# Encoder trunk on one core: gate-table eviction as a pipeline of half blocks, v's first slab ahead of the table, two half slabs of values prepared ahead

## The chip, the core and the metric

The kernel runs on one core of one Trainium2 chip. The metric is device time in microseconds for one execution, the median of three runs. TensorE (PE) multiplies, ScalarE (ACT) and VectorE (DVE) split operands and evict results, SyncE (SP) issues the loads, and ScalarE issues the stores of the gate table. In the profile's rows PEld is TensorE's weight load.

## What is computed

Two layers on a sequence of 256 tokens of width 1024 (`x` is 256 x 1024, float32): a mixer (an HGRN2 recurrence in layer 0, an RG-LRU block in layer 1), each followed by a PEER feed-forward part, which is what the change concerns:

```python
def peer_ffn(h, w_q, sub_keys, u_tab, v_tab):
    q = (h @ w_q).reshape(B, S, 8, 2, 128)
    scores = einsum('bshpd,hpkd->bshpk', q, sub_keys)
    s1, i1 = top_k(scores[..., 0, :], 16);  s2, i2 = top_k(scores[..., 1, :], 16)
    cand_s = s1[..., :, None] + s2[..., None, :]        # 256 candidates
    cand_id = i1[..., :, None] * 128 + i2[..., None, :]
    top_s, top_pos = top_k(cand_s, 16)
    ids, gate = take(cand_id, top_pos), softmax(top_s)
    # per token, 8 heads x 16 experts out of 16384
    act = gelu(einsum('thkd,td->thk', u_tab[ids], h))
    return einsum('thk,thkd->td', gate * act, v_tab[ids])
```

Every sub-layer has an RMSNorm with shift, scale and gate from a conditioning vector (adaLN).

## The kernel before, in words

The kernel gathers no rows. It computes `gelu(u h)` for all 16384 experts (the u stage), multiplies it by a dense table of gates that is zero outside the chosen experts, and multiplies the result by all of `v_tab` (the v stage). Each of `peer_u` and `peer_v` comes in 64 slabs of 1 MB (128 x 2048 float32). Float32 values are split into a high and a low part, ScalarE writing the high one (line 300) and VectorE the low one (line 301), and each product is three matmuls: 24 matmuls for half a slab in the u stage (lines 308, 309, 311), 12 in the v stage (line 1305).

*Slabs.* An arena of 19 slabs holds the u stage's activations (128 groups of 256 columns, eight groups to a slab, 16 slabs) and the incoming slabs. `order` lists all loads in the order in which they are taken; `pump()` issues the next load on SP's queue as soon as a slab is in `allowed`, and `free(n)` gives a slab back. From u slab 44 on only three slabs are left for loads, until `release` gives back slabs whose activations have been used: three at v slab 18, and in layer 0 five more at v slab 34. SP's queue is in order: a load that waits holds up those behind it.

*Products and side work.* `push(prep, mm, post, cost)` emits the preparation of a half (its split) at once and puts its matmuls into a queue that holds `depth` halves (one) back. When a half's matmuls are emitted, `side(cost)` adds `cost` to a credit and runs steps of the side generators while the credit is positive; each `yield` gives the cost of the step just emitted. In the u stage the side generators are `routing()` (scores, top-16, softmax; VectorE) and then `gmats()`, the gate table; their credit per half is C_ROUTE, then C_G0. What is left when u ends is emitted by `drain_sides()`.

*The gate table.* `gmats` works on 32 blocks of eight tokens. `build(n)` makes one-hot matrices on VectorE (lines 1204 and 1206), `mult(m)` multiplies for half a block (four matmuls, line 1215) into one of three pairs of PSUM banks, and `evict(m)` adds the two halves of the result into a staging tile STG (the tile xT, two buffers): ScalarE copies (line 1222), VectorE adds (line 1223). After a block's second half ScalarE issues the store of 512 KB to `gates` in DRAM (line 1225).

*The v stage.* Before eight v slabs, two slabs `gd` are read back from `gates` (`GLEAD` v slabs ahead; the first two at the start, which wait for the whole table, `tabled`), and `gates()` multiplies them into the activations on VectorE (line 1252). `s2` splits the v slab and one group of 256 activations for each half (lines 1296 and 1297) and multiplies. In layer 0 adaLN slabs are woven in (`ada_slab`, line 394); `load_cond` and `pre_final` broadcast columns through `row_bcast` (lines 374, 375), and `pre_final` transposes (line 1381).

Of the kernel before, what the change touches and what calls it, by code (L numbers as in the profile page):

```python
# [17 lines left out]
OP = mybir.AluOpType  # L18
# [27 lines left out]
C_ROUTE = 1.65  # L46
C_G0 = 2.05
# [25 lines left out]
def body(ctx, tc, A, out):  # L73
# [222 lines left out]

    def split(raw):
        n = wsn[0] % NWS
        wsn[0] += 1
        ACT.activation(WS[:, n, 0], raw, AF.Copy)  # L300
        V.tensor_tensor(WS[:, n, 1], raw, WS[:, n, 0], op=OP.subtract)  # L301
        return WS[:, n, 0], WS[:, n, 1]
# [85 lines left out]
    def ada_slab():  # L388
        n, raw = take("ada")
        i, s = order[n][1:]  # L390
        for m in range(2):
            col = 2 * s + m
            r_ = raw[:, m * 1024:(m + 1) * 1024]
            V.scalar_tensor_tensor(r_, r_, 1.0, cb, op0=OP.mult, op1=OP.mult, accum_out=mod[:, i, col:col + 1])  # L394
        free(n)
        if s % 4 == 3:
            c0 = 2 * (s - 3)
            V.tensor_tensor(mod[:, i, c0:c0 + 8], mod[:, i, c0:c0 + 8],
                            sv("b_ada")[:, i * 48 + c0:i * 48 + c0 + 8], op=OP.add)
            if c0 == 40:  # L400

                V.tensor_scalar(mod[:, i, c0:c0 + 8], mod[:, i, c0:c0 + 8], 1.0 / GS16, None, op0=OP.mult)

    def weaved():
        while st["taken"] < len(order) and order[st["taken"]][0] == "ada":
            ada_slab()
# [607 lines left out]
    def peer(i):  # L1014
# [179 lines left out]
        def gmats():  # L1194

            P2 = pool.tile([P, 2, NTB, 2, P], F16, name="gsplit", tag="gsplit")

            def build(n):
# [4 lines left out]
                for dst, t_ in ((EQ, T2), (P1[:, bf], T1)):  # L1203
                    V.tensor_tensor(pairs(dst), pairs(io1[:, None, :].to_broadcast([P, NTB, P])), spread(t_),  # L1204
                                    op=OP.is_equal)
# [12 lines left out]
            def evict(m):  # L1218
                b = 2 + 2 * (m % 3)
                pv = PS[:, b:b + 2].rearrange("p a (t g j) -> p g j (a t)", t=2, g=2)  # L1220
                st_ = STG[:, m // 2 % 2, :, m % 2 * 4:m % 2 * 4 + 4]
                ACT.activation(st_, pv[:, 0], AF.Copy)  # L1222
                V.tensor_tensor(st_, pv[:, 1], st_, op=OP.add)  # L1223
                if m % 2:
                    nc.scalar.dma_start(Gd[i][:, :, m // 2],
                                        STG[:, m // 2 % 2].rearrange("p (q j) t -> p q (j t)", q=8))

            for n in range(S // NTB):
                build(n)
                yield 2.7  # L1230
                if n:
                    evict(2 * n - 2)
                    yield 0.7
                mult(2 * n)
                if n:
                    evict(2 * n - 1)
                    yield 0.7
                mult(2 * n + 1)
            yield 1.0
            for m in (S // 4 - 2, S // 4 - 1):  # L1240
                evict(m)
                yield 0.7
            tabled.add(i)
            pump()

        def gates():

            n, raw = take("gd")
            q, th = order[n][2] // 2, order[n][2] % 2
            av = slabs(aslab(16 * q), 2).rearrange("p a (j t) -> p (a j) t", t=S)[:, :, th * P:(th + 1) * P].rearrange(  # L1250
                "p j (g t) -> p j g t", t=8)
            V.tensor_tensor(av, av, raw.rearrange("p (g j t) -> p j g t", g=16, t=8), op=OP.mult)  # L1252
            free(n)
# [4 lines left out]
        def s2(cost):  # L1258
            n, raw = take("v")
            g = order[n][2]  # L1260
            if g == 63 and i == 1:
# [22 lines left out]
            for half in range(2):  # L1284
# [41 lines left out]
        if i == 0:  # L1326
            sides.append(cond)
            sides.append(softplus())
        for it in vs[i]:
            if it[0] == "ada":  # L1330
                settle(cond)
                weaved()
                continue
            if it[0] == "gd":
                gates()
# [4 lines left out]
            elif g == 18:  # L1340
                release(0, 1, 2)
            elif g == 34 and i == 0:
                release(3, 4, 5, 6, 7)
            elif g == 52 and i == 0:
                reserve(0, 1, 2, 3, 4, 5, 6)
            elif g == 58 and i == 0:
                release(13)
            s2(C_G1)
            if g == 63 and i == 1:
                flush()  # L1350
            if i == 1 and g == 44:
                sides.append(pre_final())
        if i == 0:
# [156 lines left out]
```

## Time and profile before

| | |
|---|---|
| median of 3 runs | 2033.39 us (2030.5 to 2035.17) |
| profiled execution | 2030.43 us, of which its span is 2028.6 |
| granted TensorE clock, mean | 0.986 |
| busy: TensorE, VectorE, ScalarE | 1943.8, 1571.2, 1004.0 us |
| moved by DMA | 456.87 MB, 225 GB/s |
| u stages (layer 0, layer 1) | about 250 to 692, 1205 to 1647 us |
| v stages | about 692 to 1070, 1647 to 2016 us |

The span is from the first to the last instruction in the trace. An engine's busy time counts its instructions alone; TensorE's ends are modelled, so holes are read from its waits and from the starts of its matmuls.

### The profile page before, as it was taken

What the parts mean: (1) busy time and instruction counts of PE and PEld (TensorE: products, weight loads), DVE (VectorE), ACT (ScalarE), POOL (GpSimd) and SP (SyncE); (2) the same over time, 40 slices, a digit from 0 to 9 for tenths busy, and PEclk for the clock granted to TensorE, in tenths of its full rate; (3) what the DMA queues carried; (4) which work ended last, traced back from release to release, by engine and by line L of the source; (5) the groups of instructions that cost most, each with busy time, mean ns of one, the idle gap of its engine ahead of it and who ended that gap; (6) DMA issues with size and microseconds to landing.
All of it is one profiled execution on the core that took longest, in us unless ns stands there. A gap on an engine that the chain in (4) does not pass through costs nothing.

```text
span 2028.6 us, 32101 instructions
## 1 busy us (share of the span) xinstructions
PE 1943.8 (96%) x12862; PEld 1781.8 (88%) x12862; DVE 1571.2 (77%) x2797; ACT 1004.0 (49%) x1419; POOL 0.2 (0%) x4
## 2 busy tenths in 40 slices
PE   6999999999999799999999989999999979999998
PEld 6898899999999777888888889999999978888786
DVE  6798659887888677888877776988788866676575
ACT  3544544445555354444445744445455544454454
POOL 0000000000000000000000000000000000000000
PEclk9999999999999899999999999999999989999999
DMA  8654714455767667989753482545676766766561
GB/s 347 271 200 163 285 69 158 175 187 198 238 193 244 210 247 269 394 347 399 290 208 154 158 306 90 185 167 192 208 244 195 235 225 261 290 252 260 203 234 57
DMA packets 125765, 456.87 MB, mean 225 GB/s; under 512 B 7720, under 2 KB 73512, under 8 KB 74672
## 3 DMA queue, kind: packets, MB, share of 16 engines
q1 hardware_dynamic: 59056, 421.28, 55.4%
q10 hardware_dynamic: 66560, 33.56, 5.5%
q8 instruction: 100, 1.64, 0.3%
q14 instruction: 49, 0.40, 0.1%
HBM read 418.10 MB, written 36.70 MB: 224 GB/s over the span
## 4 chain that ended last, share of the span: by engine, by line
PE 88%; DVE 6%; ACT 3%; DMA 2%; issue 1%; SPq 0%; DVEq 0%; ACTq 0%
PE psum L1305 33%; PE psum L311 14%; PE psum L308 14%; PE psum L309 14%; PE psum L1215 3%; PE psum L478 2%; DVE wsplit L301 1%; PE psum L358 1%; DMA arena<-peer_v_dram 1%; PE psum L688 1%; PE psum L318 1%; PE psum L595 1%; ACT wsplit L300 1%; PE psum L1088 1%; PE psum L915 1%
## 5 line engine op out<-in xcount | busy, mean ns | idle before, releaser
L301 DVE TENSOR_TENSOR wsplit<-arena,wsplit 128x1024 fp32r<-128x1024 f32 x600 | 729.7, 1219 | 300.8 <-ACT wsplit L300 298.4
L300 ACT ACTIVATE wsplit<-arena 128x1024 fp32r<-128x1024 f32 x600 | 632.4, 1056 | 492.1 <-PE psum L1305 311.4
L1305 PE MATMUL psum<-wsplit,gsplit 128*128 128x512 f32 x3048 | 703.3, 392 | 19.4 <-ACT gsplit L1296 14.3
L1305 PEld LDWEIGHTS psum<-wsplit,gsplit 128*128 128x128 f32 x3048 | 574.8, 189 | 145.3 <-ACT gsplit L1296 15.4
L308 PE MATMUL psum<-hsplit,wsplit 128*128 128x256 f32 x2448 | 607.7, 286 | 2.1 <-ACT wsplit L300 2.1
L309 PE MATMUL psum<-hsplit,wsplit 128*128 128x256 f32 x2448 | 600.5, 283 | 0.0
L308 PEld LDWEIGHTS psum<-hsplit,wsplit 128*128 128x128 f32 x2448 | 469.1, 192 | 4.3 <-ACT wsplit L300 2.7
L309 PEld LDWEIGHTS psum<-hsplit,wsplit 128*128 128x128 f32 x2448 | 469.6, 192 | 0.1
L311 PE MATMUL psum<-hsplit,wsplit 128*128 128x256 f32 x2448 | 344.2, 283 | 2.7 <-DVE wsplit L301 2.7
L311 PEld LDWEIGHTS psum<-hsplit,wsplit 128*128 128x128 f32 x2448 | 316.5, 192 | 3.1 <-DVE wsplit L301 3.1
L1190 ACT ACTIVATE arena<-psum 128x512 f32<-128x512 f32 x128 | 76.5, 598 | 283.2 <-PE psum L311 283.2
L1223 DVE TENSOR_TENSOR xT<-psum,xT 128x512 f32<-128x512 f32 x128 | 87.6, 686 | 51.9 <-ACT xT L1222 51.9
L1297 DVE TENSOR_TENSOR gsplit<-arena,gsplit 128x256 fp32r<-128x256 f32 x254 | 105.9, 417 | 0.0
L1296 ACT ACTIVATE gsplit<-arena 128x256 fp32r<-128x256 f32 x254 | 101.4, 399 | 0.0
L394 DVE SCALAR_TENSOR_TENSOR arena<-arena,scratch 128x1024 f32<-128x1024 f32 x80 | 94.1, 1218 | 0.0
L1252 DVE TENSOR_TENSOR arena<-arena 128x2048 f32<-128x2048 f32 x32 | 71.9, 2284 | 12.2 <-DMA arena<-gates 12.2
L1222 ACT ACTIVATE xT<-psum 128x512 f32<-128x512 f32 x128 | 75.1, 589 | 8.1 <-PE psum L1215 8.1
L1206 DVE TENSOR_TENSOR gsplit<-scratch 128x2048 f16<-128x2048 f16 x64 | 78.0, 1218 | 0.0
L1215 PE MATMUL psum<-gsplit,scratch 128*128 128x256 f16 x512 | 67.0, 274 | 0.0
L1215 PEld LDWEIGHTS <-scratch 128*128 128x128 f16 x512 | 44.9, 98 | 7.1
L697 DVE TENSOR_TENSOR arena<-arena 128x512 f32<-128x512 f32 x56 | 35.7, 683 | 12.0 <-PE psum L688 6.8
L1204 DVE TENSOR_TENSOR scratch<-iota,T 128x1024 f16<-128x1024 f16 x64 | 43.8, 684 | 0.0
(219 smaller groups left out, 1258.5 us busy)
## 6 DMA issues: line engine op xcount, KB each, us to landing
arena<-peer_u_dram SPq DMA_DIRECT2D x128, 1024.0 KB, 4.9
arena<-peer_v_dram SPq DMA_DIRECT2D x128, 1024.0 KB, 4.9
arena<-w_ada_dram SPq DMA_DIRECT2D x40, 1024.0 KB, 5.9
gates<-xT ACTq DMA_DIRECT2D x64, 512.0 KB, 5.3
arena<-gates SPq DMA_DIRECT2D x32, 1024.0 KB, 4.7
arena<-w_q_dram SPq DMA_DIRECT2D x16, 1024.0 KB, 6.9
arena<-hg_k_dram SPq DMA_DIRECT2D x8, 1024.0 KB, 15.5
arena<-hg_s_dram SPq DMA_DIRECT2D x8, 1024.0 KB, 6.1
```

The source lines that it names most:

```text
L300: ACT.activation(WS[:, n, 0], raw, AF.Copy)
L301: V.tensor_tensor(WS[:, n, 1], raw, WS[:, n, 0], op=OP.subtract)
L308: PE.matmul(o, wh(k), rh(k), start=start and k == 0, stop=False)
L309: PE.matmul(o, wh(k), rl(k), start=False, stop=False)
L311: PE.matmul(o, wl(k), rh(k), start=False, stop=stop and k == ks - 1)
L394: V.scalar_tensor_tensor(r_, r_, 1.0, cb, op0=OP.mult, op1=OP.mult, accum_out=mod[:, i, col:col + 1])
L1206: V.tensor_tensor(P2[:, bf].rearrange("p t g (j z) -> p t g j z", z=2), pairs(EQ)[:, :, None].to_broadcast([P, NTB, 2, P // 2, 2]), TG[:, ...
L1215: PE.matmul(PS[:, b + t // 2, t % 2 * S:(t % 2 + 1) * S], P1[:, n % 2, 4 * h + t], P2[:, n % 2, 4 * h + t], start=True, stop=True)
L1223: V.tensor_tensor(st_, pv[:, 1], st_, op=OP.add)
L1296: ACT.activation(box_wt[0][:, z, 0], acol(j), AF.Copy)
L1297: V.tensor_tensor(box_wt[0][:, z, 1], acol(j), box_wt[0][:, z, 0], op=OP.subtract)
L1305: PE.matmul(PS[:, 4 + 2 * tb + dh], box_wt[0][:, z, a, tb * P:(tb + 1) * P], r[:, dh * 512:(dh + 1) * 512], start=(j == 0 and a == 0 and r ...
```

## The change

- `gmats` evicts as a pipeline. `step(m)` issues the store of the block that ends with half block m-3, copies half block m-1 (ScalarE), adds half block m-2 (VectorE) and multiplies half block m. A block is `build`, `step`, `step`, at costs 2.7, 0.7 and 0.7; four steps follow at the end. C_ROUTE goes from 1.65 to 1.7, C_G0 from 2.05 to 2.2.
- In `order`, v's first slab stands ahead of the first two table slabs.
- In the v stage `depth` is 2, and H (the u stage's split input) serves as two more homes for split values (`widen`, `narrow`).
- `gates()` takes two table slabs at once and leaves four multiplications of half the size (`steps_gate`); adaLN slabs are left in two parts each (`steps_ada`). `between()` runs one such step in each preparation of a half; the first half of the stage runs two.
- `row_bcast` emits the multiplications of a pair of columns one side step ahead of its matmuls. The condition's broadcast starts at v slab 4, `softplus` at v slab 20.
- Slabs are released one at a time, every four v slabs from slab 5 on.
- `row_onehots` and `by_act` are switched off (`by_act` returns False).

```diff
-C_ROUTE = 1.65
-C_G0 = 2.05
+C_ROUTE = 1.7
+C_G0 = 2.2
...
-                    if max(0, 8 * q - GLEAD) == it[2]:
+                    if q and 8 * q - GLEAD == it[2]:
                         zs += [("gd", i, 2 * q), ("gd", i, 2 * q + 1)]
             zs.append(it)
+            if it[0] == "v" and it[2] == 0:
+                zs += [("gd", i, 0), ("gd", i, 1)]
...
+    homes = [[WS[:, n] for n in range(NWS)]]
+    kept = []
+    def widen(more):
+        n = wsn[0]
+        homes.append([homes[0][(n + z) % NWS] for z in range(NWS)] + more)
+        kept.append(n)
+        wsn[0] = 0
...
     def row_bcast(cols, bank):
-        for k in range(KD):
-            V.tensor_scalar(diag[:, k % 2], ident, cols[:, k:k + 1], float(D), op0=OP.mult, op1=OP.mult)
-            PE.matmul(PS[:, bank + k // 4, k % 4 * P:(k % 4 + 1) * P], ones, diag[:, k % 2], start=True, stop=True)
-            if k % 2:
-                yield 0.8
+        for k in range(0, KD, 2):
+            for z in range(2):
+                V.tensor_scalar(diag[:, z], ident, cols[:, k + z:k + z + 1], float(D), op0=OP.mult, op1=OP.mult)
+            yield 0.8
+            for z in range(2):
+                PE.matmul(PS[:, bank + k // 4, (k + z) % 4 * P:((k + z) % 4 + 1) * P], ones, diag[:, z], start=True,
+                          stop=True)
+            yield 0.1
...
+    steps_ada, steps_gate = [], []
+    def between():
+        for xs in (steps_gate, steps_ada):
+            if xs:
+                xs.pop(0)()
+                return
...
-            def evict(m):
+            def view(m):
                 b = 2 + 2 * (m % 3)
-                pv = PS[:, b:b + 2].rearrange("p a (t g j) -> p g j (a t)", t=2, g=2)
-                st_ = STG[:, m // 2 % 2, :, m % 2 * 4:m % 2 * 4 + 4]
-                ACT.activation(st_, pv[:, 0], AF.Copy)
-                V.tensor_tensor(st_, pv[:, 1], st_, op=OP.add)
-                if m % 2:
-                    nc.scalar.dma_start(Gd[i][:, :, m // 2],
-                                        STG[:, m // 2 % 2].rearrange("p (q j) t -> p q (j t)", q=8))
+                return (PS[:, b:b + 2].rearrange("p a (t g j) -> p g j (a t)", t=2, g=2),
+                        STG[:, m // 2 % 2, :, m % 2 * 4:m % 2 * 4 + 4])
+            def step(m):
+                if m - 3 >= 0 and (m - 3) % 2:
+                    n = (m - 3) // 2
+                    nc.scalar.dma_start(Gd[i][:, :, n], STG[:, n % 2].rearrange("p (q j) t -> p q (j t)", q=8))
+                if 0 <= m - 1 < S // 4:
+                    pv, st_ = view(m - 1)
+                    ACT.activation(st_, pv[:, 0], AF.Copy)
+                if 0 <= m - 2 < S // 4:
+                    pv, st_ = view(m - 2)
+                    V.tensor_tensor(st_, pv[:, 1], st_, op=OP.add)
+                if m < S // 4:
+                    mult(m)
             for n in range(S // NTB):
                 build(n)
-                yield 2.7
-                if n:
-                    evict(2 * n - 2)
-                    yield 0.7
-                mult(2 * n)
-                if n:
-                    evict(2 * n - 1)
-                    yield 0.7
-                mult(2 * n + 1)
-            yield 1.0
-            for m in (S // 4 - 2, S // 4 - 1):
-                evict(m)
-                yield 0.7
+                yield 2.0 if by_act(n) else 2.7
+                step(2 * n)
+                yield 0.7
+                step(2 * n + 1)
+                yield 0.7
+            for m in range(S // 4, S // 4 + 4):
+                yield 0.7
+                step(m)
...
         def gates():
-            n, raw = take("gd")
+            two = [take("gd"), take("gd")]
...
+            for z in range(2):
+                for th in range(2):
+                    steps_gate.append(lambda z=z, th=th: part(z, th))
...
                     hi, lo = split(raw[:, half * 1024:(half + 1) * 1024])
                     if half == 1:
                         free(n)
+                    if j == 0:
+                        gates()
+                        between()
+                    between()
...
+        depth[0] = 2
+        widen([H[:, n].rearrange("p k t -> p (k t)").rearrange("p (a x) -> p a x", a=2) for n in range(2)])
...
-            elif g == 18:
-                release(0, 1, 2)
-            elif g == 34 and i == 0:
-                release(3, 4, 5, 6, 7)
+            if g == 20 and i == 0:
+                sides.append(softplus())
+            if g % 4 == 1 and g > 4:
+                z = g // 4 - 1
+                if z in ((0, 1, 2, 3, 4, 5, 6, 7) if i == 0 else (0, 1, 2, 7)):
+                    release(z)
```

## Rows read from the trace of the kernel before

**Rows 1.** The page, part 1: busy us, share of the span, instructions.

```profile
PE 1943.8 (96%) x12862; PEld 1781.8 (88%) x12862; DVE 1571.2 (77%) x2797; ACT 1004.0 (49%) x1419; POOL 0.2 (0%) x4
```

**Rows 2.** Stretches of 50 us: busy PE, PEld, DVE, ACT, POOL; granted clock, DMA share, GB/s.

```profile
300.00:350.00 50.00, 50.00 (x419) 50.00 (x418) 49.52 (x205) 21.98 (x27) 0.00 (x0) 1.00 0.39 141
...
550.00:600.00 50.00, 50.00 (x424) 49.14 (x423) 44.82 (x53) 26.94 (x39) 0.00 (x0) 1.00 0.63 199
...
700.00:750.00 50.00, 43.55 (x184) 34.41 (x185) 36.61 (x72) 24.94 (x38) 0.00 (x0) 0.91 0.67 257
```

**Rows 3.** TensorE's waits over the span: us in total, times, longest.

```profile
PE psum L1305 <- DVE gsplit L1297: 4.7, 5, 0.9
```

**Rows 4.** TensorE's timeline at layer 0's handover: start, us, what, idle before.

```profile
691.34 1.12 PE L311 MATMUL psum<-hsplit,wsplit 128*128 128x256 f32 x8
...
708.13 3.16 PE L1305 MATMUL psum<-wsplit,gsplit 128*128 128x512 f32 x12
...
711.49 2.98 PE L1305 MATMUL psum<-wsplit,gsplit 128*128 128x512 f32 x12
715.73 9.60 PE L1305 MATMUL psum<-wsplit,gsplit 128*128 128x512 f32 x37 [1.26 <-ACT gsplit L1296]
```

**Rows 5.** TensorE's timeline, 725 to 805 us.

```profile
724.70 63.65 PE L1305 MATMUL psum<-wsplit,gsplit 128*128 128x512 f32 x277
790.54 14.77 PE L1305 MATMUL psum<-wsplit,gsplit 128*128 128x512 f32 x57 [2.19 <-ACT gsplit L1296]
```

**Rows 6.** The chain that ended last, layer 0's handover: start, us, what.

```profile
695.17 6.69 DMA arena<-peer_v_dram
```

**Rows 7.** TensorE's timeline at layer 1's handover.

```profile
1658.59 41.60 PE L1305 MATMUL psum<-wsplit,gsplit 128*128 128x512 f32 x169 [10.90 <-ACT gsplit L1296]
```

**Rows 8.** Short stretches behind two holes, columns as in rows 2.

```profile
1660.00:1664.00 4.00, 4.00 (x11) 3.09 (x10) 2.81 (x4) 2.89 (x5) 0.00 (x0) 0.50 0.86 324
...
790.00:794.00 4.00, 3.46 (x8) 2.76 (x9) 3.38 (x5) 3.10 (x6) 0.00 (x0) 0.57 0.96 350
```

**Rows 9.** The page, parts 5 and 6: costliest groups, then DMA issues (us to landing).

```profile
L1297 DVE TENSOR_TENSOR gsplit<-arena,gsplit 128x256 fp32r<-128x256 f32 x254 | 105.9, 417 | 0.0
...
L1252 DVE TENSOR_TENSOR arena<-arena 128x2048 f32<-128x2048 f32 x32 | 71.9, 2284 | 12.2 <-DMA arena<-gates 12.2
...
arena<-peer_v_dram SPq DMA_DIRECT2D x128, 1024.0 KB, 4.9
```

**Rows 10.** TensorE's timeline, layer 1, around the last stage's transposes.

```profile
1906.88 0.60 PE L1381 MATMUL psum<-consts,xT 128*128 128x128 f32 x4
...
1924.68 3.69 PE L1305 MATMUL psum<-wsplit,gsplit 128*128 128x512 f32 x15
```

**Rows 11.** ScalarE's timeline over one block of the gate table.

```profile
659.33 0.60 ACT L1190 ACTIVATE arena<-psum 128x512 f32<-128x512 f32 x1 [1.68 <-PE psum L311]
...
661.17 0.52 ACTq L1225 DMA_DIRECT2D gates<-xT  x1
661.80 1.06 ACT L300 ACTIVATE wsplit<-arena 128x1024 fp32r<-128x1024 f32 x1 [1.38 <-DVE scratch L1204]
662.76 0.58 ACT L1222 ACTIVATE xT<-psum 128x512 f32<-128x512 f32 x1
663.24 1.05 ACT L300 ACTIVATE wsplit<-arena 128x1024 fp32r<-128x1024 f32 x1
```

**Rows 12.** DMA, 566 to 580.9 us: queue's packets, MB, share; issues.

```profile
q10 hardware_dynamic: 2259, 1.13, 26.6%
...
gates<-xT ACTq DMA_DIRECT2D x2, 512.0 KB, 3.7
```

**Rows 13.** DMA issues, 580.9 to 628 us.

```profile
gates<-xT ACTq DMA_DIRECT2D x7, 512.0 KB, 5.3
```

**Rows 14.** SP's timeline, 658 to 669 us.

```profile
659.74 6.96 SPq L212 DMA_DIRECT2D arena<-peer_u_dram  x2
```

**Rows 15.** VectorE's timeline over the same block.

```profile
658.50 1.21 DVE L301 TENSOR_TENSOR wsplit<-arena,wsplit 128x1024 fp32r<-128x1024 f32 x1
```

More of the change, by code (lines that the diff above doesn't have):

```diff
@@ L386, in load_cond, with ada_parts, ada_part @@
         cond_copy(bank)
-    def ada_slab():
+    def ada_parts():
         n, raw = take("ada")
+        return [lambda m=m: ada_part(n, raw, m) for m in range(2)]
+    def ada_part(n, raw, m):
         i, s = order[n][1:]
[L391 to L394, printed above, removed]
+        col = 2 * s + m
+        r_ = raw[:, m * 1024:(m + 1) * 1024]
+        V.scalar_tensor_tensor(r_, r_, 1.0, cb, op0=OP.mult, op1=OP.mult, accum_out=mod[:, i, col:col + 1])
+        if m == 0:
+            return
         free(n)
@@ L405, in weaved @@
         while st["taken"] < len(order) and order[st["taken"]][0] == "ada":
-            ada_slab()
+            for f in ada_parts():
+                f()
+    steps_ada, steps_gate = [], []
[3 more added lines that the diff above has]
+                xs.pop(0)()
+                return
     epst = pool.tile([P, 2], F32, name="eps")
@@ L1196, in gmats, with by_act, row_onehots @@
             P2 = pool.tile([P, 2, NTB, 2, P], F16, name="gsplit", tag="gsplit")
+            def by_act(n):
+                return False
+            def row_onehots(n, part):
+                if not by_act(n) or n >= S // NTB:
+                    return
+                if part == 2:
+                    ACT.activation(P1[:, n % 2], P1[:, n % 2], AF.Relu, scale=-1.0, bias=1.0)
+                    return
+                for t in range(4 * part, 4 * part + 4):
+                    ACT.activation(P1[:, n % 2, t], io1, AF.Abs, scale=-1.0, bias=T1[:, n * NTB + t, 0:1])
             def build(n):
@@ L1246, in gates, with part @@
         def gates():
-            n, raw = take("gd")
[L1249 to L1253, printed above, removed]
+            two = [take("gd"), take("gd")]
+            def part(z, th):
+                n, raw = two[th]
+                q = order[n][2] // 2
+                av = slab(aslab(16 * q + 8 * z)).rearrange("p (j t) -> p j t", t=S)[:, :, th * P:(th + 1) * P].rearrange(
+                    "p j (g t) -> p j g t", t=8)
+                V.tensor_tensor(av, av, raw.rearrange("p (g j t) -> p j g t", g=16, t=8)[:, 8 * z:8 * z + 8], op=OP.mult)
+                if z == 1:
+                    free(n)
+            for z in range(2):
+                for th in range(2):
+                    steps_gate.append(lambda z=z, th=th: part(z, th))
         box_wt = []
@@ L1260, in s2 @@
             g = order[n][2]
+            while g % 8 == 0 and g and steps_gate:
+                steps_gate.pop(0)()
             if g == 63 and i == 1:
@@ L1325, in peer @@
         cond = load_cond(2)
[L1326 to L1329, printed above, removed]
+        depth[0] = 2
+        widen([H[:, n].rearrange("p k t -> p (k t)").rearrange("p (a x) -> p a x", a=2) for n in range(2)])
+        for n, it in enumerate(vs[i]):
             if it[0] == "ada":
                 settle(cond)
-                weaved()
+                steps_ada.extend(ada_parts())
                 continue
             if it[0] == "gd":
-                gates()
+                if it[2] and it[2] % 2 == 0:
+                    gates()
                 continue
@@ L1339, in peer @@
                 nc.sync.dma_start(XT, Xd[i])
[L1340 to L1344 removed]
+                if i == 0:
+                    sides.append(cond)
+            if g == 20 and i == 0:
[4 more added lines that the diff above has]
+                    release(z)
+            if g == 52 and i == 0:
                 reserve(0, 1, 2, 3, 4, 5, 6)
@@ L1352, in peer @@
                 sides.append(pre_final())
+        narrow()
+        while steps_ada:
+            steps_ada.pop(0)()
         if i == 0:
```

19 lines of the change are left out of this document (14 added, 5 removed).

## The prediction

> **What bounds the kernel.** I read the page first: TensorE is busy for 96% of the span [rows 1]. The stretches of 50 us then show where the other 4% lie: in the u stage TensorE has no idle time at all (50.00 of 50, 424 matmuls), at the handover from u to v it has 43.55 of 50 [rows 2]. Its waits [rows 3] and its timeline give each hole a place and a size:
>
> - Handover, layer 0: the last u product ends at 692.46 (691.34 + 1.12), unbroken v work starts at 715.73 [rows 4]. Between lie two half slabs of v (24 matmuls of 0.23 us, which is 63.65 / 277 [rows 5], so 5.5 us) and 16 small broadcast matmuls (0.15 each, like the transposes of [rows 10], 2.4 us): 23.3 - 5.5 - 2.4 = 15.4 us lost. The chain shows why: the loads of gates and of v stand on SP's queue behind the table's last store, and v's slab, issued at 695.17, lands 6.69 us later [rows 6].
> - Handover, layer 1: 10.90 us idle, then 169 matmuls in 41.60 us instead of 38.8 [rows 7], since the granted clock is 0.50, TensorE's 1.2 GHz level, after the idle time [rows 8]: 13.7.
> - At 788 us: 2.19 idle, then 57 matmuls in 14.77 instead of 13.1 [rows 5], at a granted clock of 0.57 [rows 8]: 3.9.
> - Five stalls behind the gating of activations, which takes VectorE two lumps of 2.28 us every eight v slabs [rows 9]: 4.7 together [rows 3].
> - Layer 1, 1906.88 to 1924.68, transposes and broadcast of the last stage: 17.8 - 36 x 0.23 - 32 x 0.15 = 4.7 [rows 10].
>
> So the change can gain at most 42 us, all in v's two stages. In the u stages it can only lose.
>
> **Part by part: the gains.** *Earlier table.* By the costs in the code, routing asks for 103.6 of credit and the table for 132.2; at 1.65 and 2.05 per half product that is 62.8 + 64.5 = 127 of 128 halves. At 1.7 and 2.2, with 134.0 for the new table, it is 60.9 + 60.9 = 122. The last store leaves some five halves earlier, and v's first slab stands ahead of the table on SP's queue. What is late next? Three slabs are free there. One holds v's first slab, the two table slabs take the others, and the second of them is issued when the last u slab has been split, about 6 us (two halves) before u ends. It lands after 4.9, like a v slab [rows 9]; one more gating step of 1.14 (half of 2.28) and ScalarE's copy follow: first v product about 0.5 late. v's second slab can be loaded only after the first is split, and that split stands behind the copy on ScalarE: issued 2.7 us into v, landed after 4.9, split and copied by 9.0, while the first slab's products end at 6.0: 3 lost. VectorE's gating step and subtraction behind that split hold the next matmuls for another 1.4. Sum 5; with 2 for a lower clock afterwards, as after the hole of 2.19 us [rows 8], each handover keeps 7. Gain 15.4 - 7 = 8.4 and 13.7 - 7 = 6.7.
>
> *Gates and adaLN slabs in parts.* Such a step now stands behind a half: VectorE has 1.21 + 0.42 + 1.14 = 2.8 us [rows 9, 15] in a half of 2.76 (12 x 0.23), and 1.6 in one without; two half slabs prepared ahead level that out. Slabs come free one by one from the sixth v slab on (before: three at once at the nineteenth), so six instead of three are there at 788. Gain 4.7 + 3.9; if that cover is gone, these 8.6 stay.
>
> *Broadcast, softplus, homes.* The multiplications of a broadcast run a side step ahead; of layer 1's 4.7 I leave 0.7 for transposes that wait for their own eviction; gain 4.0. Softplus only moves. The extra homes for split values lie in H, which the last u product frees; the first split into it is the fourth half of v: no wait. The one-hot code for ScalarE is switched off and costs nothing.
>
> Gains: 8.4 + 6.7 + 4.7 + 3.9 + 4.0 = 28 us; 42 at most, and 22 if the handovers keep 10 each.
>
> **Part by part: what the pipeline adds.** The staging tile has two buffers. Block n is copied into one in steps 2n+1 and 2n+2, added to in 2n+2 and 2n+3, and its store is now issued in step 2n+4; step 2n+5 begins with ScalarE's copy of block n+2 into the same buffer. Before, three evictions lay between a store and that copy. Now it is one step, and the copy must wait until the store has landed. ScalarE works in order: behind the copy stand the split of the next half, a GELU, another split and then the next store; TensorE waits for the splits. This is a ring: landing, copy 0.48, split 0.96, GELU 0.60, split 0.96, store [rows 11], which is 3.0, plus the store's own time to land. TensorE's round of two halves and one block is 56 matmuls, 6.6 us (50 x 56 / 424 [rows 2]).
>
> How long does a store take? 3.7 us with no load beside it, 5.3 with one [rows 12, 13]. In the latter the u slab's load is issued at 659.74, the store at 661.17, 1.43 later [rows 14, 11]: the 512 KB wait behind the 1 MB. The load leaves when VectorE has split the second half of a slab (658.50 + 1.21 = 659.71 [rows 15]). So its place in the ring decides.
>
> Counting the credit (2.2 in per half; 2.7, 0.7, 0.7 out), 30 stores of a layer have such a copy behind them. For 21 both steps fall behind the same half, for 9 behind two. Of the 21, 11 fall behind the first half of a slab, 10 behind the second (two runs of five: halves 73 to 81 and 101 to 109).
>
> - Behind a first half, the slab is freed by the second split of the ring: its load leaves 0.48 + 0.96 + 1.05 + 1.22 = 3.7 after the landing, the store at 3.0. The store goes first and takes 3.7: ring 6.7 against 6.6. Nothing lost.
> - Behind a second half, it is freed by the first split: the load leaves at 0.48 + 1.05 + 1.22 = 2.8, 0.2 ahead of the store. The store then waits almost the whole load out: 5.3 + 1.43 - 0.2 = 6.5, ring 9.5, 2.9 over TensorE's round. The first round of each run is covered by the lead of the splits; four pay: 11.6, both runs 23.
> - Divided ones have a split and perhaps the GELU inside the store's time, so they lack up to 1.6 of the 3.0: not over TensorE's round by more than the lead covers.
>
> So 23 us per layer, 46 in all. Bounds: every store at 3.7, 21 x 0.1 = 2 per layer; every store at 5.3, 21 x 1.7 = 36 per layer. I take 23, since the order of issue fixes which stores meet a load.
>
> A rule speaks on this point. The Trainium skill, "DMA: Bandwidth & Descriptors", section "Queues, rings and completion order", says that each DMA engine takes turns between the queues that have work for it, a packet at a time. By it a store beside a load does not wait the load out, and the sum is that of the second rival; 3.7 against 5.3 us alone does not tell the two apart.
>
> *Routing at 1.7:* VectorE is busy for 49.52 of 50 us there while TensorE stays unbroken [rows 2], so 0.05 more per half over some 20 halves can cost up to 1 us in each of four stretches; splits are done ahead, and I take 0.
>
> **Sum.** -28 + 46 = +18. The profiled execution took 2030.4 (span 2028.6 and 1.8 around it), so 2048; the median of the runs is 3.0 above it, and 18 on the median gives 2051.
>
> **Rivals.**
> - *Stores never meet a load*, because the load leaves behind the store: 2 us per layer, -28 + 4 = -24, 2009. For it: 0.2 us decides the order. Against it: the load's issue needs VectorE alone, which stands idle then. Its point: a load over some tenths behind the store. Faster than before; 0.32.
> - *The DMA engines take turns.* The store's own transfer (26.6% of 14.9 us for 1.13 MB, so 1.8 us for 512 KB [rows 12]) takes twice as long beside a load: 3.7 + 1.8 = 5.5, ring 8.5, 1.9 over; 8 such rounds, 15 per layer: -28 + 30 = +2, 2035. For it only that nothing in these rows excludes it; 0.14. This is the Trainium skill's rule from above.
> - *The handovers are not better*, since v's second slab waits for the gates' slabs: their 15 us come back to the 18, 2066; 0.04, beside the forecast.
>
> **How the numbers follow.** The forecast has 0.50, at 2051; by its own bounds 2037 (16 per layer) to 2077 (36). 2012 to 2070 leaves out the far part of the first rival and the upper end of the forecast, about 2 in 10. Less than 0.2% (4 us) cannot be told from no change here. Faster: the first rival and a little of the second, 0.33; same: most of the second, 0.12; slower: 0.55.
>
> **What the profile after would show.** Right: a new wait of ScalarE for the store into the gates in the u stages; TensorE below 50 of 50 there, most of it in two runs of halves per layer; a hole of 4 to 8 us at the handover; no five stalls in layer 0. Wrong: TensorE unbroken in the u stages (then 2009), stores landing after 3.7 throughout, or a hole of over 10 us at the handover.

## The result, and the profile after

The changed kernel takes 2014.64 us, median of 4 runs (2011.72 to 2015.77), against 2032.74 for the kernel before on the same chip: ratio 0.9915, 95% interval 0.9900 to 0.9929, faster by 0.85%. I had forecast 2051, slower. The profiled execution has a span of 2013.6 us, 15.0 below that of before.

The page of the changed kernel, parts 1 and 6 (columns as in [rows 1, 9]):

```profile
PE 1944.6 (97%) x12862; PEld 1782.8 (89%) x12862; DVE 1584.6 (79%) x2829; ACT 1005.1 (50%) x1419; POOL 0.2 (0%) x4
...
gates<-xT ACTq DMA_DIRECT2D x64, 512.0 KB, 3.8
```

Stretches of 50 us of the changed kernel, for [rows 2] (its v stage of layer 0 begins at 701 us, 9 later than before):

```profile
300.00:350.00 50.00, 50.00 (x418) 49.92 (x417) 49.59 (x209) 22.66 (x26) 0.00 (x0) 1.00 0.36 127
550.00:600.00 50.00, 49.59 (x418) 48.17 (x417) 44.91 (x55) 26.61 (x38) 0.00 (x0) 1.00 0.61 198
600.00:650.00 50.00, 47.26 (x395) 45.65 (x394) 43.32 (x54) 25.17 (x37) 0.00 (x0) 1.00 0.70 228
700.00:750.00 50.00, 46.47 (x203) 37.53 (x203) 33.22 (x47) 24.17 (x37) 0.00 (x0) 0.93 0.66 247
750.00:800.00 50.00, 50.00 (x223) 41.40 (x222) 41.14 (x53) 25.92 (x38) 0.00 (x0) 1.00 0.88 344
```

Waits over the span: in place of the five stalls of [rows 3] there are these.

```profile
ACT xT L1278 <- DMA gates<-xT: 79.1, 32, 4.6
PE psum L1263 <- DVE xT L1281: 8.4, 13, 1.1
PE psum L1374 <- ACT gsplit L1365: 5.3, 2, 2.7
PE psum L325 <- ACT wsplit L317: 3.4, 5, 1.0
PE psum L1263 <- DVE gsplit L1254: 1.4, 3, 0.5
```

Two signs of the forecast are there: TensorE, unbroken in the u stages before, is not so now, and ScalarE's copy (line 1278) waits for the stores 32 times. A third is not: TensorE's holes do not lie in two runs of halves, layer 0 has nine between 486 and 668 us. And TensorE hardly waits for the splits, as I had it (line 317: 3.4 us in five waits, against 2.1 in three for line 300 of the kernel before). What is new in the u stages is nearly all at the multiplications for the gate table (line 1263), which wait for VectorE's additions (8.4 us) and for its building of one-hot matrices (1.4). Of the signs of being wrong, "stores landing after 3.7 throughout" comes close, with a median of 3.8. I measure each stage between starts in TensorE's timeline: u from the first score matmul (line 1088 before, 1123 after) to the last matmul of a u product, v from there to the last matmul of a v product. Layers 0 and 1:

| kernel | median, us | u | v |
|---|---|---|---|
| before | 2032.74 | 401.4, 401.4 | 378.1, 367.2 |
| the change | 2014.64 | 408.6, 409.7 | 357.2, 355.8 |

The v stages gain 20.9 and 11.4, together 32.3 (forecast 28). The u stages lose 7.2 and 8.3, together 15.5 (forecast 46). That is 16.8; the opening of the program, whose first score matmul starts between 288.4 and 294.5 us in the profiles of this study, took 1.8 longer in this one.

The handover of layer 0 in TensorE's timeline, for [rows 4]:

```profile
701.28 5.79 PE L1374 MATMUL psum<-wsplit,gsplit 128*128 128x512 f32 x24
709.68 1.65 PE L1374 MATMUL psum<-wsplit,gsplit 128*128 128x512 f32 x4 [2.61 <-ACT gsplit L1365]
712.10 3.78 PE L1374 MATMUL psum<-wsplit,gsplit 128*128 128x512 f32 x8 [0.77 <-DVE gsplit L1366]
715.68 6.28 PE L1374 MATMUL psum<-hsplit,gsplit 128*128 128x512 f32 x24
```

The 15.4 us ahead of v are gone; two holes behind the products of its first slab remain, 3.4 us together, and behind them 8 matmuls take 3.78 us (from 712 to 716 us the granted clock is 0.50, the 1.2 GHz level, in the row below).

```profile
712.00:716.00 4.00, 3.90 (x9) 3.13 (x10) 4.00 (x6) 1.86 (x4) 0.00 (x0) 0.50 0.81 276
```

### The profile page after: what moved, and what is told of

Same layout as the page of the kernel before. It is cut to its first block, busy times and chain, and to the rows that moved or that the text cites. A ratio compares the mean times of both kernels' runs of the same rounds, so it can differ in the third digit from the quotient of the medians.

```text
span 2013.6 us, 32138 instructions
## 1 busy us (share of the span) xinstructions
PE 1944.6 (97%) x12862; PEld 1782.8 (89%) x12862; DVE 1584.6 (79%) x2829; ACT 1005.1 (50%) x1419; POOL 0.2 (0%) x4
## 4 chain that ended last, share of the span: by engine, by line
PE 79%; DVE 10%; ACT 4%; DMA 4%; issue 2%; ACTq 0%; DVEq 0%; SPq 0%
PE psum L1374 34%; PE psum L325 11%; PE psum L328 11%; PE psum L326 11%; DVE wsplit L318 3%; DMA gates<-xT 3%; PE psum L513 2%; ACT wsplit L317 2%; PE psum L1263 2%; PE psum L375 1%; PE psum L723 1%; PE psum L335 1%; DVE arena L581 1%; DVE xT L1281 1%; DVE gsplit L1254 1%
## 5 line engine op out<-in xcount | busy, mean ns | idle before, releaser
L318 DVE TENSOR_TENSOR wsplit<-arena,wsplit 128x1024 fp32r<-128x1024 f32 x500 | 606.5, 1219 | 237.7 <-ACT wsplit L317 235.4
L317 ACT ACTIVATE wsplit<-arena 128x1024 fp32r<-128x1024 f32 x500 | 521.7, 1051 | 88.3 <-PE psum L326 33.4
L1374 PE MATMUL psum<-wsplit,gsplit 128*128 128x512 f32 x1848 | 434.5, 393 | 6.4 <-ACT gsplit L1365 5.3
L1374 PEld LDWEIGHTS psum<-wsplit,gsplit 128*128 128x128 f32 x1848 | 348.8, 189 | 81.2 <-ACT gsplit L1365 6.1
L1374 PE MATMUL psum<-hsplit,gsplit 128*128 128x512 f32 x1200 | 281.9, 390 | 0.0
L1374 PEld LDWEIGHTS psum<-hsplit,gsplit 128*128 128x128 f32 x1200 | 226.0, 189 | 47.0
L1365 ACT ACTIVATE gsplit<-arena 128x256 fp32r<-128x256 f32 x254 | 105.7, 416 | 294.2 <-PE psum L1374 271.7
L318 DVE TENSOR_TENSOR hsplit<-arena,hsplit 128x1024 fp32r<-128x1024 f32 x100 | 122.4, 1224 | 26.3 <-ACT hsplit L317 25.6
L317 ACT ACTIVATE hsplit<-arena 128x1024 fp32r<-128x1024 f32 x100 | 104.6, 1046 | 8.3 <-DMA arena<-peer_v_dram 8.3
L1263 PE MATMUL psum<-gsplit,scratch 128*128 128x256 f16 x512 | 72.4, 274 | 9.8 <-DVE xT L1281 8.4
```

What stands on the lines that cost most here:

```text
L317: ACT.activation(w_[:, 0], raw, AF.Copy)
L318: V.tensor_tensor(w_[:, 1], raw, w_[:, 0], op=OP.subtract)
L1263: PE.matmul(PS[:, b + t // 2, t % 2 * S:(t % 2 + 1) * S], P1[:, n % 2, 4 * h + t], P2[:, n % 2, 4 * h + t], start=True, stop=True)
L1365: ACT.activation(box_wt[0][:, z, 0], acol(j), AF.Copy)
L1374: PE.matmul(PS[:, 4 + 2 * tb + dh], box_wt[0][:, z, a, tb * P:(tb + 1) * P], r[:, dh * 512:(dh + 1) * 512], start=(j == 0 and a == 0 and r ...
```

## Where the ring of the prediction breaks

ScalarE's timeline of the changed kernel; ACTq is the moment at which the engine issues a DMA:

```profile
517.73 0.60 ACT L1278 ACTIVATE xT<-psum 128x512 f32<-128x512 f32 x1 [3.31 <-DMA gates<-xT]
517.90 0.52 ACTq L1275 DMA_DIRECT2D gates<-xT  x1
518.23 1.05 ACT L317 ACTIVATE wsplit<-arena 128x1024 fp32r<-128x1024 f32 x1
519.17 0.59 ACT L1225 ACTIVATE arena<-psum 128x512 f32<-128x512 f32 x1
519.65 1.06 ACT L317 ACTIVATE wsplit<-arena 128x1024 fp32r<-128x1024 f32 x1
520.60 0.59 ACT L1278 ACTIVATE xT<-psum 128x512 f32<-128x512 f32 x1
```

In the program's order these six are: copy (waits for the store before), split, GELU, split, *store*, copy. The splits, the GELU and the next copy run in that order. The store, fifth, leaves second, 0.17 us after the waiting copy has started, and not 3.0 after it. The chain of waits of the same kernel shows the ring as it is in this round, the store's 5.20 us and then 0.1 and a little:

```profile
512.45 5.20 DMA gates<-xT
517.65 0.02 issue
517.69 0.04 issue
517.73 0.10 ACT xT L1278
517.83 0.07 issue
517.90 0.52 ACTq L1275
518.42 0.86 ACT wsplit L317
...
519.31 1.23 DVE wsplit L318
...
524.01 0.61 DVE xT L1281
...
524.66 0.60 PE psum L1263 x4
```

5.4 us fits in TensorE's round of 6.6. The later rows show how a late copy still reaches TensorE here: ScalarE's split comes late behind it, VectorE's split and building behind that, and at their end the addition (line 1281) that a multiplication waits for. Three theories were put to the test. Theory 1: the store is issued once the waits of all instructions ahead of it are met, though ScalarE has not yet done their work, and what the u stages still lose comes from the two buffers. Theory 2: only the order of loads and stores on the DMA engines counts. Theory 3: the loss comes from the credits of 1.7 and 2.2.

## The experiments

In this table u and v are measured as above, layers 0 and 1, and the ratios are to the kernel before, run on the same chip (2032.6 to 2033.5).

| run | median, us | ratio (95%) | u | v |
|---|---|---|---|---|
| e1_tied | 2126.38 | 1.0463 (1.0446 to 1.0481) | 466.8, 461.5 | 357.2, 355.4 |
| e2_third | 2006.06 | 0.9868 (0.9852 to 0.9885) | 404.7, 404.7 | 357.4, 356.6 |
| e3_old_evict | 2007.59 | 0.9876 (0.9860 to 0.9893) | 405.3, 405.3 | 357.2, 356.2 |
| e4_old_credit | 2044.14 | 1.0061 (1.0045 to 1.0078) | 416.7, 415.5 | 364.4, 363.3 |
| e5_third_credit | 2027.50 | 0.9981 (0.9971 to 0.9990) | 409.3, 409.3 | 364.4, 362.9 |
| e6_v_alone | 2013.80 | 0.9919 (0.9902 to 0.9935) | 401.4, 401.4 | 365.1, 364.0 |
| e7_xt_slab | 1991.78 | 0.9807 (0.9791 to 0.9823) | 404.6, 404.6 | 350.5, 349.3 |
| e8_depth1 | 2016.25 | 0.9915 (0.9900 to 0.9930) | 408.5, 409.7 | 358.4, 357.3 |
| e9_store_step | 2020.60 | 0.9946 (0.9930 to 0.9963) | 411.8, 413.6 | 357.4, 355.6 |
| e11_order | 2018.60 | 0.9926 (0.9911 to 0.9941) | 409.1, 409.7 | 358.0, 357.4 |
| e12_early_add | 1991.11 | 0.9796 (0.9782 to 0.9809) | 404.3, 404.3 | 350.5, 349.3 |
| e13_tied_third | 2007.42 | 0.9872 (0.9856 to 0.9887) | 404.7, 404.7 | 357.5, 356.6 |

**e1_tied: the store is made to wait for ScalarE's work.**

```diff
                     n = (m - 3) // 2
+                    one = STG[:, n % 2, 0:1, 0:1]
+                    ACT.activation(one, one, AF.Copy)
                     nc.scalar.dma_start(Gd[i][:, :, n], STG[:, n % 2].rearrange("p (q j) t -> p q (j t)", q=8))
```

> A copy of one element of the staging buffer onto itself, by ScalarE, stands in front of each store, so that the store can be issued only when ScalarE has done the splits and the GELU before it in its order. Theory 1 (the u stages lose 15 to 17 us because a copy waits until the store before it has landed, and they lose no more because the next store is issued ahead of ScalarE's queued work): the ring becomes the landing time plus up to 3.0 us, as in the prediction, and the u stages lose 30 to 46 us instead of 17: 2027 to 2044. Theory 2 (only the order of loads and stores on the DMA engines sets the loss, whatever stands behind the copy): stores are a little later, 2010 to 2020. Theory 3 (the loss comes from the credit of 1.7 and 2.2, which puts more VectorE work in a half): 2014 to 2016, with ScalarE's 64 extra copies hidden.

Measured 2126, far beyond even theory 1. Here TensorE does wait for the splits, and ScalarE's timeline shows why:

```profile
PE psum L325 <- ACT wsplit L317: 52.2, 30, 4.6
```

```profile
528.14 0.60 ACT L1280 ACTIVATE xT<-psum 128x512 f32<-128x512 f32 x1 [5.86 <-DMA gates<-xT]
528.64 1.05 ACT L317 ACTIVATE wsplit<-arena 128x1024 fp32r<-128x1024 f32 x1
529.59 0.59 ACT L1225 ACTIVATE arena<-psum 128x512 f32<-128x512 f32 x1
530.06 1.06 ACT L317 ACTIVATE wsplit<-arena 128x1024 fp32r<-128x1024 f32 x1
531.01 0.20 ACT L1276 ACTIVATE xT<-xT 128x1 f32<-128x1 f32 x1
531.24 0.52 ACTq L1277 DMA_DIRECT2D gates<-xT  x1
531.81 0.60 ACT L1280 ACTIVATE xT<-psum 128x512 f32<-128x512 f32 x1 [0.60 <-ACT xT L1276]
538.50 0.60 ACT L1280 ACTIVATE xT<-psum 128x512 f32<-128x512 f32 x1 [6.09 <-DMA gates<-xT]
```

This is the prediction's ring, link by link: copy, split, GELU, split, and the store 3.10 us after the copy (forecast 3.0). The u slab's load is issued by SP at 530.97, 0.27 ahead of it (forecast 0.2), and the next copy is released 7.26 after the store (forecast 6.5): a ring of 10.36 (forecast 9.5). So every link was right but the one that the change does not have. The size differs too, 60 to 65 us per layer over before instead of 23. Rounds that I had let go free pay too: where the load leaves 0.68 behind the store (SP 562.34, store 561.66), the copy is released 6.67 us after the store, not 3.7, and the next store leaves at 570.48, a ring of 8.82.

**e2_third and e13_tied_third: a third buffer.** The third is half of arena slab 18.

```diff
+        S3 = [STG[:, 0], STG[:, 1], slab(18)[:, 1024:2048].rearrange("p (j t) -> p j t", t=NTB)]
...
-                        STG[:, m // 2 % 2, :, m % 2 * 4:m % 2 * 4 + 4])
+                        S3[m // 2 % 3][:, :, m % 2 * 4:m % 2 * 4 + 4])
...
+            if n == 26:
+                reserve(18)
```

> A third staging buffer, half a slab of the arena that the last activations use only at the end; the loads have one slab fewer from u slab 26 on instead of 44. Theory 1: a copy now has one more round of 6.6 us before its buffer must be empty, more than any store takes to land, so ScalarE no longer waits for a store; the u stages lose 2 to 4 us instead of 17, and the time is 1999 to 2003. Theory 2 (the stores themselves, by what they do to the loads, hold TensorE up): the stores stay, and loads have a slab less, 2013 to 2020. Theory 3 (credit): 2013 to 2016.

Measured 2006.06: no copy waits for a store any more, and the u stages gain 3.9 and 5.0 on the change. Theory 1 has the direction and theory 2 falls, but 3.3 us per layer stay, 6.6 in all where I expected 2 to 4, and the time is 3 us above my range. With the tie added to three buffers:

> The tied store (a copy of one element of the staging buffer onto itself by ScalarE ahead of each store) with three staging buffers. With two it took 2126 us, with three and no tie 2006. Theory 1 (the tie costs because the next copy into the same buffer waits for the late store, a ring through ScalarE's splits): with a third buffer the ring has a round more, and the time is 2006 to 2011. Rival (the extra copies themselves hold ScalarE and the splits up): most of the 112 us stay, above 2050.

Measured 2007.42, as theory 1 has it: the u stages are those of e2_third (404.7) and the medians 1.4 us apart, within the intervals. So the 112 us between e1_tied and the change do not come from the tied copies themselves but from what waits behind a late store.

**e3_old_evict: the eviction of before, all else as changed** (`evict` and its yields in place of `step`).

> The changed kernel with the eviction of before (copy, add and store in one step) at the new credits, all else as changed. Theory 1: no copy waits for a store, since three evictions lie between a store and the copy into its buffer; the u stages lose 0 to 3 us, and the v stages keep their gain of 32: 1997 to 2002. Theory 2: the number and size of the stores are the same, 2010 to 2016. Theory 3: 2013 to 2016. If the early start of v needed the pipeline, the handovers lose what they gained: 2010 to 2018 with TensorE unbroken in the u stages.

Measured 2007.59: 7 us better than the change, so the pipeline is a loss where it stands. Not the 1997 to 2002 of theory 1: the u stages lose 3.9 each without any wait for a store, in four holes of TensorE per layer: three in which a multiplication for the table waits for an addition, as in the change, and a smaller one at a split.

**e4_old_credit and e5_third_credit: the old credits.**

```diff
-C_ROUTE = 1.7
-C_G0 = 2.2
+C_ROUTE = 1.65
+C_G0 = 2.05
```

> The changed kernel with the credits of before, 1.65 and 2.05 per half product. The table then asks for 62.8 + 65.4 = 128.2 halves of 128, so its last steps fall behind the end of u. Theory 1: the waits for stores stay (a block comes every 2.00 halves instead of 1.86, 7.1 us instead of 6.6, so some rings fit): u loses 8 to 17, but the handovers lose most of their 15, since the gates come back late: 2015 to 2030. Theory 3: the u stages lose nothing, the handovers as above: 2008 to 2013.

> The third staging buffer with the credits of before, 1.65 and 2.05. With the third buffer alone each u stage still lost 3.3 us, in six holes of 0.5 us in which the second multiplication of a block waits for an addition. Theory 1 (these come from the credit of 2.2, by which two steps often fall behind one half): at 2.05 a block takes exactly two halves, the u stages are as before, 401.4 us from the scores on, but the table is late and each v stage begins some 9 us late and is some 7 us longer in all, as with the old credits and two buffers: 2006 - 6.6 + 14 = 2013. Theory 2 (the stores beside the loads hold TensorE up whatever the buffers): u stages of 405 us or more: 2019 to 2025.

Measured 2044.14 and 2027.50. Theory 3 falls: the u stages of e4 are worse, not better, and worse than theory 1 had it too. 58 copies wait for a store there, 147.9 us in all. At 2.05 a block takes exactly two halves, and the store's place among them is the same in every round. ScalarE's timeline of e4_old_credit:

```profile
597.40 0.60 ACT L1278 ACTIVATE xT<-psum 128x512 f32<-128x512 f32 x1 [2.38 <-DMA gates<-xT]
597.89 2.00 ACT L317 ACTIVATE wsplit<-arena 128x1024 fp32r<-128x1024 f32 x2
601.21 0.60 ACT L1225 ACTIVATE arena<-psum 128x512 f32<-128x512 f32 x1 [1.31 <-PE psum L328]
601.21 0.52 ACTq L1275 DMA_DIRECT2D gates<-xT  x1
```

The two splits are done at 599.89. The GELU ahead of the store waits for TensorE until 601.21, and the store leaves with its start, not with its end. So the store is not free: it runs ahead of work, but not ahead of a wait. The third buffer takes 13.6 us of e4's loss away, but my expectation of e5 failed too: with three buffers and the old credits I expected 401.4 us of u and got 409.3. Theory 2 has the nearer time, but not the cause: no store of e5 has its last packet more than 5 us after issue, and what TensorE waits for is the addition. TensorE's waits in e5_third_credit, and under them those of e2_third:

```profile
PE psum L1265 <- DVE xT L1283: 7.0, 22, 0.3
PE psum L1265 <- DVE arena L1283: 3.2, 10, 0.3
```

```profile
PE psum L1265 <- DVE xT L1283: 3.3, 10, 0.3
PE psum L1265 <- DVE arena L1283: 0.7, 2, 0.3
```

That is 32 waits in two layers at 2.05 and 12 at 2.2. Between starts of matmuls each hole is 0.59 to 0.61 us where 0.11 is usual, so 0.5 lost: 16 x 0.5 = 8 per layer in e5 (measured 7.9) and 6 x 0.5 = 3 in e2 (3.3). In each, the second multiplication of a block waits for an addition. In the code one `yield` lies between the addition that frees a PSUM pair and the multiplication that takes it, two before; where both steps fall behind the same half, the addition can come too late. All the holes lie in such rounds, but not every such round has one: 6 of 23 per layer in e2, every second of 32 in e5, where at 2.05 all rounds are of this kind. What decides between them stays open.

**e12_early_add: that addition ahead of the building of the block** (on top of e7_xt_slab).

```diff
+                if n:
+                    add(2 * n - 2)
                 build(n)
```

> The third buffer and the table slab in xT, and the addition of a block's second last half, which frees the PSUM banks that the next block's second multiplication needs, stands ahead of VectorE's building of that block instead of behind it. Theory 1 (the six holes of 0.5 us left in each u stage arise where both steps of a block fall behind one half, because that addition comes 0.6 us after the end of the building): the holes go, the u stages are as before, 401.5 instead of 404.6 us from the scores on: 1991.8 - 6.4 = 1985 to 1986. Rival (the holes come from ScalarE's copy, which the addition waits for): VectorE then builds later instead, 1990 to 1996.

Measured 1991.11, not different from e7_xt_slab. The six holes of a layer are gone; four, of 0.73 between starts, are there instead, in rounds whose two steps fall behind different halves, and in them the first multiplication waits for the building (line 1265). VectorE's and TensorE's timelines at one of them:

```profile
542.50 0.69 DVE L1284 TENSOR_TENSOR xT<-psum,xT 128x512 f32<-128x512 f32 x1 [0.73 <-ACT xT L1293]
545.59 0.61 PE L1274 MATMUL psum<-gsplit,scratch 128*128 128x256 f16 x4 [0.46 <-DVE gsplit L1265]
```

This is the rival's outcome and, in the four rounds of layer 0, its mechanism: the addition now stands ahead of the building, VectorE waits 0.7 us in it for ScalarE's copy, and the building comes later by that much. What would remove these last 3 us per layer stays open.

**e9_store_step: only the store goes back to the step of its addition.**

```diff
                     V.tensor_tensor(st_, pv[:, 1], st_, op=OP.add)
+                    if m % 2:
+                        store((m - 2) // 2)
```

> The pipeline with two buffers, but each store is issued in the step of its last addition, a step earlier than in the change. Theory 1 (the copy waits because only one step lies between the store and the copy into its buffer): the store leaves up to a step earlier, the copy's wait shrinks, and the u stages lose 3 to 5 us each instead of 7 to 8: 2007 to 2011. Rival (ScalarE now waits at the store for VectorE's addition, which costs as much as it gains): 2013 to 2020. Rival (the stores meet the loads more often): above 2020.

Measured 2020.60, on the border between the two rivals, and the trace has signs of both. ScalarE's wait for stores shrinks from 79.1 to 32.8 us, but what stands behind the store on ScalarE now waits for VectorE's addition (line 1280, 12 times, at the splits), and TensorE's multiplications wait 20 times for VectorE's additions instead of 13. And 15 of 64 stores have their last packet more than 5 us after issue, against 6 in the change. Which of the two costs more stays open.

**e6_v_alone: eviction and credits of before, v part as changed.**

> The v part of the change alone: eviction and credits of before, but v's first slab ahead of the table, depth 2, gating and adaLN in parts, the new releases and broadcasts. Theory 1 (the v stages' gain has two parts, of which the handovers need the earlier table): u stages as before, 401.4 us; v stages of some 364 us as with the old credits, against 378 and 367 before: 14 + 4 gained, 2015. Rival (the handover's gain comes from the order of the loads alone): v stages of 357 us, 2001. Rival (nothing of the gain is left without the table's being early): 2030.

Measured 2013.80, no different from the whole change. The early table is worth 7.9 and 8.2 us in v (365.1 to 357.2 and 364.0 to 355.8), and the pipeline with its credits costs 15.5 in u. It is the credits that bring the early table: with them and the old eviction, e3_old_evict has the v stages of the change.

**e11_order and e8_depth1: parts of the v stage undone.**

```diff
-                    if q and 8 * q - GLEAD == it[2]:
+                    if max(0, 8 * q - GLEAD) == it[2]:
...
-            if it[0] == "v" and it[2] == 0:
-                zs += [("gd", i, 0), ("gd", i, 1)]
```

> The change, but v's first slab stands behind the first two table slabs on SP's queue, as before. Theory 1 (with the table ready early, v's first slab is then the load issued when the last u slab has been split, 6 us before u ends, and lands after 5 to 6 us, is split in 2): v begins 2 to 4 us late in each layer, 2018 to 2023. Rival (the order makes no difference, since all three loads have to be there): 2013 to 2016. Rival (as before, some 15 us per layer): 2035 or more.

Measured 2018.60: v's first product starts 3.1 us after the start of the last u matmul instead of 0.13, in both layers. Part of that is won back, the v stages are only 0.8 and 1.6 us longer, and the interval of the time overlaps that of the change. For e8_depth1 the line `depth[0] = 2` is left out:

> The change with one half slab of values prepared ahead in the v stage instead of two; gating in parts, homes and releases as changed. Theory 1 (a part of the gating makes VectorE's work of a half 2.8 us against TensorE's 2.76, and the second half slab ahead levels that out): the five stalls of before come back in part, and the v stages lose 3 to 8 us: 2018 to 2023. Rival (the gating in parts alone took the stalls away): 2013 to 2016.

Measured 2016.25, not different from the change within the intervals; the v stages are 1.1 and 1.5 us longer in the profile, and no stall of before comes back. So the second half slab ahead is not what removed the stalls. The division of the gating is what is left of my reason, but the additional homes and the new releases stayed in this run, and no run undoes the division alone.

**e7_xt_slab: the second table slab goes into xT** (on top of e2_third). The tile is empty from the last store until the residual is read back.

```diff
+            if order[n][0] == "gd" and order[n][2] == 1:
+                if order[n][1] not in tabled:
+                    return
+                held[n] = "xT"
+                nc.sync.dma_start(XT.rearrange("p k t -> p (k t)"), src(order[n]))
+                st["issued"] += 1
+                continue
```

> The third buffer, and in addition the second table slab is loaded into the tile xT, which is the staging tile until the last store and is free then until the residual is read back at v slab 4; so v's second slab can be loaded as soon as the last u slab has been split. Theory 1 (the hole of 2.6 to 3 us behind v's first half and the half clock after it come from the slab that v's second slab has to wait for): both go, about 3 + 1.2 + 2 us in each layer, 1994 to 1997. Rival (the hole is VectorE's gating of the first activations, whatever the loads): 2004 to 2006. Rival (three loads at once hold each other up, so that v's first product is late): above 2006.

Measured 1991.78. TensorE's timeline at its handover of layer 0, for [rows 4]:

```profile
693.19 8.51 PE L1387 MATMUL psum<-wsplit,gsplit 128*128 128x512 f32 x36
701.54 5.60 PE L1387 MATMUL psum<-hsplit,gsplit 128*128 128x512 f32 x24
706.98 5.60 PE L1387 MATMUL psum<-wsplit,gsplit 128*128 128x512 f32 x24
```

No hole and no half clock: 36 matmuls in 8.35 us between starts, 0.23 each, and the v stages are 6.9 and 7.3 us shorter than in e2_third. This version is 1.9% faster than before and 1.1% faster than the change.

## Why the prediction was wrong

*The failed step* is in the sentence "ScalarE works in order: behind the copy stand the split of the next half, a GELU, another split and then the next store", from which came "a ring: landing, copy 0.48, split 0.96, GELU 0.60, split 0.96, store". The program's order is that, and the engine works in that order, but the issue of a store is not held by the engine's work. In layer 0 of the change the two runs of five rounds that I had billed stand at 518 to 545 and 609 to 636 us. There 7 of the 10 stores leave 0.0 to 0.2 us after the start of the copy before them and the others 0.9 to 1.7, not 3.0, and the u slab's load leaves 1.2 to 3.5 behind the store, not 0.2 ahead. In other rounds something ahead of the store does wait: of the 32 rounds in both layers whose copy waited for a store, 11 have the next store 0.1 to 0.3 after the copy, 18 have it 2.4 to 4.0 after, in 16 of these with the GELU waiting for TensorE. e1_tied shows that with the 3.0 us put back the ring is there, 10.36 where I had 9.5. "TensorE waits for the splits" failed with it: in the change it waits nearly always at the multiplications for the table, for VectorE's additions. Term by term: 46 us for both layers; measured 15.5, of which 8.9 go with the two buffers (e2_third) and 6.6 stay with three buffers, in multiplications that wait for VectorE's additions, which I had not foreseen, since I counted the copy's new place and not the addition's.

*A second step was wrong, but did not decide the result*: "The store goes first and takes 3.7". In e1_tied a load 0.68 us behind the store made that 6.67.

*The rival that came nearest*, "stores never meet a load" (2009), has the right sign and comes within 6 us, for another reason, and partly by luck: it had 4 us for the pipeline where 15.5 were measured, and gains of 28 where 32.3 were. In the change 6 of 64 stores have their last packet more than 5 us after issue, in e1_tied 30. The load does leave behind the store, as that rival says, but because the store leaves when the copy is released, well ahead of the split that frees the slab.

*Right:* the handover ("each handover keeps 7": e7_xt_slab removes the two holes and the half clock and gains 6.9 and 7.3; v's second slab is issued at 703.47, 2.2 into v, where I had 2.7). The gate stalls and the 788-us stall are gone, from 750 to 800 us TensorE is busy for all of 50; no run undoes the new releases, so what removed the latter is not shown. The gains in all: 28 forecast, 32.3 measured; 3.9 of the difference lies in layer 0. The reason given for the gate stalls was half wrong, as e8_depth1 shows. The routing at 1.7 costs nothing that shows: from 300 to 350 us TensorE is unbroken as in [rows 2].

## What to carry to other kernels

When a DMA is issued by an engine that computes, cost its place by the waits ahead of it, not by the work ahead of it. Set the time that a store takes beside a load against the time until its staging buffer is written again, here 5 to 7 us against a round of 6.6: with two buffers copies waited, and a third took all of that wait away. And when steps are spread over halves by a credit, look at the rounds in which two of them fall behind one half: in the change, e2_third and e5_third_credit all the waits for additions sit there, though e12_early_add moved them to other rounds.

## What was not expected of the hardware

*Two ways in which a store and a load share the DMA engines.* In e1_tied, the load issued 0.27 us ahead of the store: from 533 to 535 us the packets are the load's alone, and of the store's 1040 packets 964 move from 536 to 538.6. By queue (q1 SP's loads, q10 ScalarE's stores; packets, MB, share of the engines), first 533 to 535, then 536 to 538.6:

```profile
q1 hardware_dynamic: 88, 0.72, 96.5%
...
q10 hardware_dynamic: 964, 0.49, 62.8%
q1 hardware_dynamic: 10, 0.02, 1.7%
...
q10 hardware_dynamic: 526, 0.27, 48.8%
q1 hardware_dynamic: 60, 0.49, 48.1%
```

The last pair is the stretch from 563.4 to 566, with the load 0.68 behind the store: both move, each with half of the engines' time. These are not single cases: in all 16 rounds of e1_tied with the load 0.27 ahead the store's first packet comes 4.3 to 4.5 us after its issue, and in all 14 with the load 0.68 behind 1.2 after. The Trainium skill, "DMA: Bandwidth & Descriptors", section "Queues, rings and completion order", has the engines go round between the queues that have work, a packet at a time. In the second case both queues move as it says (48.8% of the time beside 48.1%), though the trace's packets do not go one for one (526 beside 60). In the first 88 packets go to none; the trace does not tell whether the store's packets stood in the queue by then, so whether the rule fails there is not shown. Why a load that is ahead holds the store up until it is nearly done was not tried.

*ScalarE's issue of a store runs ahead of its work* by 2.7 us here (517.90 against 520.60, when ScalarE had all but done the splits and the GELU ahead of it), and it is held by an instruction ahead of it whose wait is not met (in e4_old_credit until 601.21).
